# Down projection of a SwiGLU layer: a fourth quarter of the first pair's columns computed with seven block products instead of eight

## The chip, the cores and the metric

The kernel runs on one core of one Trainium2 chip. The metric is the time of one execution on the device in microseconds (us), the median of the runs; the reference's inputs and outputs are float32. A profile of one execution shows what every engine did: TensorE (PE, matmuls; PEld its weight loads), VectorE (DVE), ScalarE (ACT), GpSimd (POOL) and SyncE (SP, which here only starts transfers).

## The reference

One layer on x of 256 rows by 2048 columns. It has five parts, of which two are alike and concern the change:

```
x = x + 0.5 * swiglu(rms_norm(x, ffn1_norm), w_gate, w_up, w_down)     # first half FFN
...                                                                    # S5 state space and stick-breaking attention, one projection out
x = x + 0.5 * swiglu(rms_norm(x, ffn2_norm), w_gate, w_up, w_down)     # second half FFN
...                                                                    # gated embedding

def swiglu(h, w_gate, w_up, w_down):
    return (silu(h @ w_gate) * (h @ w_up)) @ w_down
```

The hidden width of an FFN is 5632, so the down projection is a product of 256 x 5632 by 5632 x 2048.

## The kernel before

**How a product is made exact enough.** TensorE multiplies float32 data in a rounded form ("fp32r"). Each operand is split into a rounded part and a remainder: ScalarE casts (hi), VectorE subtracts (lo), in `split` (lines 182 and 185). A product is hi*hi + lo*hi + hi*lo, so three matmuls for each 128 rows of the sum. The activations are the stationary operand (128x128), the weights the moving one (128 rows by 512 columns).

**How the down projection is tiled.** The sum over 5632 goes in eleven "k quarters" of 512 rows, numbered 0 to 10. The 2048 columns go in four blocks of 512, taken in two pairs (`for n in range(0, ND, 2)`): first the pair of blocks 0 and 1, then 2 and 3. The 256 rows of the activations are two tiles of 128. So a quarter and a pair form a 2x2 by 2x2 product of blocks: two row tiles and two halves of the quarter (256 rows each) against those two halves and two column blocks. There are two ways to compute it, both of class `Seven` (line 501):

- `column` (line 660), "c" in a plan: eight block products, four for each column block. Each weight tile of a quarter (raw, 128x2048) is loaded by SP (line 343), split in two halves, and every half is multiplied with both row tiles. 48 matmuls of 128x512, four splits of weights.
- `chunk` (line 635), "s" in a plan: seven block products after Winograd's form of Strassen's scheme. Both weight tiles are loaded (line 557); VectorE forms three sums of their blocks (`add`, line 550); one more sum is made in place by an adding transfer that POOL starts (line 643); seven splits follow, and 42 matmuls (lines 539, 542, 544). On the side of the activations it needs four sums of the quarter's blocks, made by `sum_forms` (line 487): four VectorE operations of 128x256 (line 496) and one split of 128x1024. A plan's "f" makes those sums ahead of their use.

The products of "c" are added up in banks 2 and 4 (first column block) and 3 and 8 (second); those of "s" in the same and in the shared banks 1, 5, 6 and 7. After the pair's last "s", `opened` (line 811) reads the shared banks: one copy on ScalarE (line 814), and on VectorE two additions (lines 815 and 820) and six gathers into x (line 809). After the pair's last quarter, `end` (line 846) gathers banks 2 and 4, then 3 and 8 into x, and the next norm's `block` transposes x on VectorE (line 220).

**What sets the order.** A plan per pair, in `plans` (line 824), written by hand, gives the order of the quarters. The instructions are then placed on the engines' queues by the framework's scheduler, which also moves them within the limits of the data. Every engine works through its own queue in order. Buffers turn around in pools: five raw tiles, of which x holds two in this stage; four pairs whi/wlo and three pairs shi/slo for split weights (`weight_pair`, line 316, takes them alternately); two for a quarter's split activations (`halves("h")`, tiles hhi and hlo, held by `kept`); four for the split sums of activations and for the next norm's output (`halves("n")`, tiles nhi and nlo); two for sums (tag "sum"). VectorE and ScalarE work ahead of TensorE as far as these pools allow.

**Which sums are kept.** `summed` (line 839) returns a quarter's sums of activations, made at first use. In the first pair (n = 0) the sums for 0 are given back after use, the others are kept for the second pair; in the second pair all are given back.

The two FFNs run the same code, so both down stages follow the same plans.

Of the kernel before, what the change touches and what calls it, by code (L numbers as in the profile page):

```python
# [33 lines left out]
def layer_kernel(ctx: ExitStack, tc: tile.TileContext, a: dict, shapes: dict, out: bass.AP):  # L34
# [47 lines left out]
    def small(n=8):  # L82
        return smp.tile([P, 8], F32, tag="sm", name=uid("sm"))[:, :n]
# [391 lines left out]
    def whole_rows(pool, parts, pinned=False):  # L475

        hi, lo = parts
        u = pool.tile([P, 2, NB], F32, tag="sum", name=uid("whole"), bufs=2)
        added = nc.vector.tensor_tensor(
            out=u.rearrange("p j n -> p (j n)"), in0=hi.bitcast(F32).rearrange("p j t -> p (j t)"),  # L480
            in1=lo.bitcast(F32).rearrange("p j t -> p (j t)"), op=ALU.add,
        )
        if pinned:
            pin(added)
        return u.rearrange("p j n -> p (j n)").rearrange("p (j x b) -> p j x b", j=4, b=32)

    def sum_forms(pool, u, kind="n"):

        sums = pool.tile([P, 2, NB], F32, tag="sum", name=uid("rows"), bufs=2)
        s = sums.rearrange("p j n -> p (j n)").rearrange("p (z j x b) -> p z j x b", z=4, j=2, b=32)  # L490
        (a11, a21), (a12, a22) = ([u[:, k : k + 2, 4 * t : 4 * t + 4] for t in range(TT)] for k in (0, 2))
        for z, (x, y, op) in enumerate((
            (a21, a22, ALU.subtract), (s[:, 0], a11, ALU.subtract),
            (a11, a21, ALU.subtract), (a12, s[:, 1], ALU.add),
        )):
            nc.vector.tensor_tensor(out=s[:, z], in0=x, in1=y, op=op)
        both = halves(kind)
        split(*both, sums.rearrange("p j n -> p (j n)").rearrange("p (z t) -> p z t", z=4))
        return both
# [175 lines left out]
    def ffn(i, xn, nxt, bg=None):  # L675
# [26 lines left out]
        for f in range(NF):  # L702
# [9 lines left out]
            if f >= early or f in alone:  # L712
# [17 lines left out]
                s = Seven(xn, lambda kb: sums[kb], ((wg, f * NB), (wu, f * NB)), sevens, turns)  # L730
# [69 lines left out]
        def rows(k):  # L800
            return hT[k // 2][:, k % 2 * 4 : k % 2 * 4 + 4]
# [9 lines left out]
        def opened(s, n):  # L811
# [10 lines left out]
            gather(xt[1][n + 1], one, -0.5)  # L822

        plans = (
            (("c", 3), ("c", 4), ("s", 0), ("c", 5), ("c", 6), ("s", 1), ("c", 7), ("c", 8), ("s", 2), ("c", 9), ("c", 10)),
            (
                ("c", 10), ("c", 9), ("s", 2), ("c", 3), ("s", 1), ("f", 0), ("c", 4), ("s", 0), ("a", (5, 6, 7, 8)),
            ),
# [1 line left out]
        parts, forms = {}, {}  # L830
# [8 lines left out]
        def summed(kb):  # L839
            if kb not in forms:  # L840
                forms[kb] = sum_forms(sevens, rows(kb))
            return forms.pop(kb) if kb == 0 or n else forms[kb]

        for n in range(0, ND, 2):

            def end(side):
                m = n + side
                for t, z in enumerate(((2, 4), (3, 8))[side]):
                    gather(xt[t][m], s.bank(z), 0.5)
                put_off(0 if m == ND - 2 or m == ND - 1 and m < nxt.early else 2, nxt.block, m)  # L850

            s = Seven(kept, summed, ((wd, n * NB), (wd, (n + 1) * NB)), sevens, turns)
            plan = plans[n // 2]
            left = sum(kind == "s" for kind, _ in plan)
            for kind, kb in plan:
                final = (kind, kb) == plan[-1]
                if kind == "f":
                    forms[kb] = sum_forms(sevens, rows(kb))
                    continue
                if kind == "s":  # L860
                    left -= 1
                    s.chunk(kb, () if left else shared)
                    if not left:
                        put_off(0, opened, s, n)
                    continue
                for side in range(2):
                    s.column(side, (kb,) if kind == "c" else kb[:: 1 - 2 * side], final)
                    if final:
                        end(side)
# [738 lines left out]

    n1, nm, n2, npl = Normed("ffn1_norm", load_turned), Normed("mix_norm"), Normed("ffn2_norm", kinds="hhnn", late=0), Normed("ple_norm", late=0)
    ffn(1, n1, nm, s5_prep)  # L1610

    w_in = a["w_in"]
# [6 lines left out]
    forms = {}  # L1619
# [68 lines left out]
    mix.close()  # L1688

    ffn(2, n2, npl)  # L1690


# [62 lines left out]
    with sums_phase("sums3") as sevens:  # L1755
        forms = {1: sum_forms(sevens, whole_rows(sevens, npl(1)), "h")}
        s = Seven(npl, forms.get, ((wg, 0), (wg, NB)), sevens, sevens)
# [16 lines left out]
    n = ND - 1  # L1774
# [14 lines left out]
    s = small(1)  # L1789
# [157 lines left out]
```

## Time and profile before

| | |
|---|---|
| median of 3 runs | 1810.87 us (1810.7 to 1810.97) |
| the profiled execution | 1810.19 us, of which 1808.4 us from the first to the last instruction |
| granted clock of TensorE | 1.00 |
| first down stage, both pairs | about 472 to 703 us |
| second down stage, both pairs | about 1471 to 1702 us |
| read from HBM / written | 372.41 MB / 10.88 MB |

Times in the profile are microseconds from the span's start. A row of a timeline has the start, the length, the engine, the line, the operation with its result and operands by the program's names, shapes, and, in brackets, how long the engine stood idle before it and who ended that. A row of waits has who waited for whom, the sum, how often and the longest. Matmuls overlap in the profile, so the time one costs is read from start to start. In the names, "acc" and "aux" are banks of TensorE's results; whi/wlo and shi/slo are split weights; sum, weight sums; rows, the sums of activations; mid, the transposed x.

### The profile page before, as it was taken

How to read it: one execution, taken by the hardware profiler on the slowest of the kernel's cores; microseconds unless marked ns; L12 is line 12 of the kernel's file. 1: busy time of each engine (PE TensorE's matmuls, PEld its weight loads, DVE VectorE, ACT ScalarE, POOL GpSimd, SP SyncE). 2: the span in 40 equal slices, each digit the busy share in tenths (PEclk: the TensorE clock that was granted, in tenths of full speed). 3: DMA queues.
4: the chain of work that ended last, by engine and by line, in shares of the span. 5: the costliest groups of instructions: out<-in, count | busy, mean ns of one | idle time of the engine just before them, and what ended most of it. 6: DMA issues, size and time to landing. Idle time of an engine off the chain costs nothing.

```text
span 1808.4 us, 24260 instructions
## 1 busy us (share of the span) xinstructions
PE 1802.4 (100%) x8902; PEld 1494.8 (83%) x8902; DVE 1598.6 (88%) x1872; ACT 1077.4 (60%) x1255; POOL 132.4 (7%) x194
## 2 busy tenths in 40 slices
PE   9999999999999999999999999999999999999998
PEld 8888888888888888888898888888888888888887
DVE  7998889999998897887767899999999999889875
ACT  7545456556565665466895666555565656556664
POOL 0020100000000001122121000000000000000000
PEclk9999999999999999999999999999999999999999
DMA  9689967787776666765646777776777786666663
GB/s 378 213 277 321 276 219 236 244 271 217 252 278 209 207 231 225 249 242 184 205 148 210 246 278 244 258 259 227 233 232 252 237 270 243 223 207 221 203 245 128
DMA packets 108232, 429.46 MB, mean 237 GB/s; under 512 B 24561, under 2 KB 48401, under 8 KB 65713
## 3 DMA queue, kind: packets, MB, share of 16 engines
q1 hardware_dynamic: 95952, 390.10, 61.1%
q0 software_dynamic: 11872, 37.50, 9.6%
q8 instruction: 70, 1.15, 0.3%
q14 instruction: 50, 0.40, 0.1%
q10 hardware_dynamic: 288, 0.31, 0.1%
HBM read 372.41 MB, written 10.88 MB: 212 GB/s over the span
## 4 chain that ended last, share of the span: by engine, by line
PE 99%; DVE 0%; issue 0%; POOL 0%; ACT 0%; DVEq 0%; POOLq 0%
PE acc L358 32%; PE acc L353 16%; PE aux L358 15%; PE aux L353 8%; PE acc L539 5%; PE acc L544 5%; PE acc L542 5%; PE aux L542 3%; PE aux L544 3%; PE aux L539 3%; PE aux L1325 0%; PE acc L1582 0%; PE acc L1577 0%; PE acc L1573 0%; PE aux L1270 0%; PE aux L252 0%
## 5 line engine op out<-in xcount | busy, mean ns | idle before, releaser
L185 DVE TENSOR_TENSOR wlo<-raw,whi 128x1024 fp32r<-128x1024 f32 x478 | 577.6, 1223 | 99.0 <-ACT whi L182 94.1
L182 ACT CAST whi<-raw 128x1024 fp32r<-128x1024 f32 x478 | 495.4, 1050 | 274.0 <-PE acc L358 150.7
L358 PE MATMUL acc<-whi,nhi 128*128 128x512 f32 x852 | 332.7, 392 | 0.1
L358 PE MATMUL acc<-whi,nlo 128*128 128x512 f32 x852 | 330.6, 390 | 0.0
L353 PE MATMUL acc<-wlo,nhi 128*128 128x512 f32 x852 | 241.4, 390 | 0.0
L185 DVE TENSOR_TENSOR slo<-raw,shi 128x1024 fp32r<-128x1024 f32 x186 | 226.8, 1219 | 16.2 <-ACT shi L182 15.6
L182 ACT CAST shi<-raw 128x1024 fp32r<-128x1024 f32 x186 | 195.4, 1050 | 62.1 <-DMA raw<-in_ffn_w_down 24.3
L358 PEld LDWEIGHTS acc<-whi,nhi 128*128 128x128 f32 x852 | 159.9, 188 | 34.1 <-issue 0.5
L353 PEld LDWEIGHTS acc<-wlo,nhi 128*128 128x128 f32 x852 | 159.7, 188 | 33.7 <-DVE wlo L185 0.3
L358 PEld LDWEIGHTS acc<-whi,nlo 128*128 128x128 f32 x852 | 160.0, 188 | 32.5
L182 ACT CAST whi<-sum 128x1024 fp32r<-128x1024 f32 x79 | 83.3, 1054 | 158.3 <-DVE sum L550 141.6
L182 ACT CAST shi<-sum 128x1024 fp32r<-128x1024 f32 x59 | 62.2, 1054 | 102.2 <-DVE sum L550 95.3
L643 POOL DMA_DIRECT2D raw<-raw x45 | 39.2, 871 | 1042.3 <-DVE sum L550 737.6
L550 DVE TENSOR_TENSOR sum<-sum,raw 128x1024 f32<-128x1024 f32 x92 | 112.4, 1222 | 0.9
L185 DVE TENSOR_TENSOR wlo<-sum,whi 128x1024 fp32r<-128x1024 f32 x79 | 96.5, 1223 | 4.8 <-ACT whi L182 4.1
L358 PE MATMUL aux<-whi,nhi 128*128 128x512 f32 x244 | 95.1, 390 | 0.0
L358 PE MATMUL aux<-whi,nlo 128*128 128x512 f32 x244 | 95.0, 389 | 0.0
L353 PE MATMUL aux<-wlo,nhi 128*128 128x512 f32 x244 | 75.2, 389 | 0.0
L185 DVE TENSOR_TENSOR slo<-sum,shi 128x1024 fp32r<-128x1024 f32 x59 | 72.1, 1223 | 1.2 <-ACT shi L182 0.5
L358 PE MATMUL acc<-whi,hlo 128*128 128x512 f32 x156 | 60.9, 390 | 0.0
L358 PE MATMUL acc<-whi,hhi 128*128 128x512 f32 x156 | 60.7, 389 | 0.0
L550 DVE TENSOR_TENSOR sum<-raw,raw 128x1024 f32<-128x1024 f32 x46 | 56.2, 1222 | 3.7 <-DMA raw<-in_ffn_w_down 3.7
(420 smaller groups left out, 3533.3 us busy)
## 6 DMA issues: line engine op xcount, KB each, us to landing
raw<-in_ffn_w_down SPq DMA_DIRECT2D x88, 1024.0 KB, 4.9
raw<-in_ffn_w_gate SPq DMA_DIRECT2D x87, 1024.0 KB, 7.1
raw<-in_ffn_w_up SPq DMA_DIRECT2D x87, 1024.0 KB, 5.4
raw<-in_w_in SPq DMA_DIRECT2D x32, 1024.0 KB, 5.1
raw<-raw POOLq DMA_DIRECT2D x48, 512.0 KB, 5.9
raw<-in_w_out SPq DMA_DIRECT2D x16, 1024.0 KB, 4.9
raw<-in_w_ple_gate SPq DMA_DIRECT2D x16, 1024.0 KB, 5.1
hT<-mid SPq DMA_DIRECT2D x160, 64.0 KB, 4.5
```

What stands on the lines that cost most here:

```text
L182: copy = nc.scalar.copy(hi, src)
L185: rest = nc.vector.tensor_tensor(out=lo, in0=src, in1=hi.bitcast(F32), op=ALU.subtract)
L353: nc.tensor.matmul(ps[t], lhsT=lh, rhs=lo[:, j, cols], start=False, stop=stop and j == 1)
L358: nc.tensor.matmul(ps[t], lhsT=(ahi, alo)[i][:, 2 * h + j, t * P : (t + 1) * P], rhs=hi[:, j, cols], start=start and j == 0 and i == 0, st ...
L539: nc.tensor.matmul(ps, lhsT=lh[j], rhs=hi[:, j], start=begin and j == 0, stop=False, skip_group_check=joined)
L542: nc.tensor.matmul(ps, lhsT=ll[j], rhs=hi[:, j], start=False, stop=False, skip_group_check=joined)
L544: nc.tensor.matmul(ps, lhsT=lh[j], rhs=lo[:, j], start=False, stop=z in final and j == 1, skip_group_check=joined)
L550: nc.vector.tensor_tensor(out=t, in0=x, in1=y, op=ALU.add)
L643: nc.gpsimd.dma_start(b12, b22, accum_op=ALU.add)
```

## The change

The first pair's plan has a fourth "s": quarter 9 is computed with seven products instead of eight. The third "s", quarter 2, comes one quarter sooner, ahead of quarter 8. The sums of activations for 9 are made (by an "f") ahead of quarter 8, and given back after use, as only the first pair uses them. The second pair's plan and everything else stay.

```
         plans = (
-            (("c", 3), ("c", 4), ("s", 0), ("c", 5), ("c", 6), ("s", 1), ("c", 7), ("c", 8), ("s", 2), ("c", 9), ("c", 10)),
+            (
+                ("c", 3), ("c", 4), ("s", 0), ("c", 5), ("c", 6), ("s", 1), ("c", 7), ("s", 2), ("f", 9), ("c", 8), ("s", 9),
+                ("c", 10),
+            ),
...
         def summed(kb):
             if kb not in forms:
                 forms[kb] = sum_forms(sevens, rows(kb))
-            return forms.pop(kb) if kb == 0 or n else forms[kb]
+            return forms.pop(kb) if n or kb in (0, 9) else forms[kb]
```

The three added lines move all later lines of the file by three. Now what it moves on the engines, in the first FFN. First the loads of weights that SP starts, from quarter 7 of the first pair to quarter 10; line 343 loads a tile for a "c", line 557 for an "s". Before:

```order
L343 DMA raw_4747<-in_ffn_w_down 128x2048
L343 DMA raw_4781<-in_ffn_w_down 128x2048
L343 DMA raw_4819<-in_ffn_w_down 128x2048
L343 DMA raw_4853<-in_ffn_w_down 128x2048
L557 DMA raw_4887<-in_ffn_w_down 128x2048
L557 DMA raw_4889<-in_ffn_w_down 128x2048
L343 DMA raw_4985<-in_ffn_w_down 128x2048
L343 DMA raw_5029<-in_ffn_w_down 128x2048
L343 DMA raw_5067<-in_ffn_w_down 128x2048
L343 DMA raw_5103<-in_ffn_w_down 128x2048
```

The same place now:

```order
L343 DMA raw_4747<-in_ffn_w_down 128x2048
L343 DMA raw_4781<-in_ffn_w_down 128x2048
L557 DMA raw_4815<-in_ffn_w_down 128x2048
L557 DMA raw_4817<-in_ffn_w_down 128x2048
L343 DMA raw_4922<-in_ffn_w_down 128x2048
L343 DMA raw_4956<-in_ffn_w_down 128x2048
L557 DMA raw_4990<-in_ffn_w_down 128x2048
L557 DMA raw_4992<-in_ffn_w_down 128x2048
L343 DMA raw_5079<-in_ffn_w_down 128x2048
L343 DMA raw_5125<-in_ffn_w_down 128x2048
```

The number of loads stays; the two of quarter 2 come ahead of quarter 8's, and quarter 9's two are a group's now.

Then VectorE after the last split of quarter 7. Before, quarter 8 begins here: raw_4819 and raw_4853 are its tiles, hT_715 its activations, raw_4887 and raw_4889 those of quarter 2.

```order
L185 TENSOR_TENSOR wlo_4822<-raw_4819,whi_4821 128x1024
L185 TENSOR_TENSOR hlo_4816<-hT_715_3976,hhi_4815 128x1024
L185 TENSOR_TENSOR slo_4826<-raw_4819,shi_4825 128x1024
L185 TENSOR_TENSOR wlo_4856<-raw_4853,whi_4855 128x1024
L185 TENSOR_TENSOR wlo_4860<-raw_4853,whi_4859 128x1024
L185 TENSOR_TENSOR slo_4908<-raw_4887,shi_4907 128x1024
L550 TENSOR_TENSOR sum_4904<-raw_4887,raw_4889 128x1024
```

Now quarter 2 is being worked on there (raw_4815 and raw_4817), and these are the rows from its third sum to the first split of quarter 8 (raw_4922); rows_4909 are the sums of activations for quarter 9:

```order
L550 TENSOR_TENSOR sum_4867<-sum_4855,raw_4815 128x1024
L185 TENSOR_TENSOR slo_4880<-raw_4815,shi_4879 128x1024
L496 TENSOR_TENSOR rows_4909<-hT_715_3976 128x256
L185 TENSOR_TENSOR wlo_4870<-sum_4867,whi_4869 128x1024
L185 TENSOR_TENSOR wlo_4890<-raw_4817,whi_4889 128x1024
L496 TENSOR_TENSOR rows_4909<-rows_4909,hT_715_3976 128x256
L496 TENSOR_TENSOR rows_4909<-hT_715_3976 128x256
L496 TENSOR_TENSOR rows_4909<-hT_715_3976,rows_4909 128x256
L185 TENSOR_TENSOR slo_4900<-raw_4817,shi_4899 128x1024
L185 TENSOR_TENSOR nlo_4915<-rows_4909,nhi_4914 128x1024
L185 TENSOR_TENSOR hlo_4919<-hT_715_3976,hhi_4918 128x1024
L185 TENSOR_TENSOR wlo_4925<-raw_4922,whi_4924 128x1024
```

The sums for 9 stand among the last splits of group 2.

Last, VectorE around the end of the first pair. x_4231 and x_4232 are the two row tiles of x; acc_4255 and acc_4262 are banks 2 and 4, aux_4291 banks 3 and 8; raw_5179, raw_5221 and raw_5259 before are the second pair's tiles of quarter 10 (second column block) and of quarter 9.

```order
L185 TENSOR_TENSOR slo_5186<-raw_5179,shi_5185 128x1024
L809 SCALAR_TENSOR_TENSOR x_4231<-acc_4255,x_4231 128x512
L220 STREAM_TRANSPOSE mid_5163<-x_4231 128x4x4x32
L809 SCALAR_TENSOR_TENSOR x_4232<-acc_4262,x_4232 128x512
L185 TENSOR_TENSOR wlo_5224<-raw_5221,whi_5223 128x1024
L220 STREAM_TRANSPOSE mid_5163<-x_4232 128x4x4x32
L185 TENSOR_TENSOR wlo_5228<-raw_5221,whi_5227 128x1024
L809 SCALAR_TENSOR_TENSOR x_4231<-aux_4291,x_4231 128x512
L809 SCALAR_TENSOR_TENSOR x_4232<-aux_4291,x_4232 128x512
L220 STREAM_TRANSPOSE mid_5163<-x_4231 128x4x4x32
L220 STREAM_TRANSPOSE mid_5163<-x_4232 128x4x4x32
L185 TENSOR_TENSOR slo_5262<-raw_5259,shi_5261 128x1024
```

Now, with raw_5201 in the place of raw_5179 and raw_5243 in that of raw_5221:

```order
L185 TENSOR_TENSOR wlo_5204<-raw_5201,whi_5203 128x1024
L809 SCALAR_TENSOR_TENSOR x_4232<-sg_5101,x_4232 128x512 x2
L809 SCALAR_TENSOR_TENSOR x_4231<-acc_4255,x_4231 128x512
L809 SCALAR_TENSOR_TENSOR x_4232<-acc_4262,x_4232 128x512
L220 STREAM_TRANSPOSE mid_5185<-x_4231 128x4x4x32
L220 STREAM_TRANSPOSE mid_5185<-x_4232 128x4x4x32
L185 TENSOR_TENSOR slo_5208<-raw_5201,shi_5207 128x1024
L185 TENSOR_TENSOR wlo_5246<-raw_5243,whi_5245 128x1024
L809 SCALAR_TENSOR_TENSOR x_4231<-aux_4291,x_4231 128x512
L809 SCALAR_TENSOR_TENSOR x_4232<-aux_4291,x_4232 128x512
L220 STREAM_TRANSPOSE mid_5185<-x_4231 128x4x4x32
L220 STREAM_TRANSPOSE mid_5185<-x_4232 128x4x4x32
```

The last split of the second pair's quarter 10 (slo_5208) stood ahead of the gathers and stands behind the first two of them; the second split of the first tile of quarter 9 (before wlo_5228, ahead of the last two gathers) comes behind them too.

## The prediction

> **What bounds the kernel now.** The first view is the page: its header, the busy times, and the chain of work that ended last.
>
> ```profile
> span 1808.4 us, 24260 instructions
> PE 1802.4 (100%) x8902; PEld 1494.8 (83%) x8902; DVE 1598.6 (88%) x1872; ACT 1077.4 (60%) x1255; POOL 132.4 (7%) x194
> PE 99%; DVE 0%; issue 0%; POOL 0%; ACT 0%; DVEq 0%; POOLq 0%
> ```
>
> TensorE is busy for the whole span and the chain lies on it: a matmul taken away is time taken away, as long as TensorE never has to wait for its operands. VectorE at 88% is the engine that can make it wait. Busy matmuls overlap in the profile, so prices come from start to start. The second view is the timeline of TensorE in the first down stage: the first matmul of quarters 7, 8, 2 (as seven products), 9 and 10.
>
> ```profile
> 534.67 0.39 PE L358 MATMUL acc<-whi,hhi 128*128 128x512 f32 x1
> 545.55 0.39 PE L358 MATMUL acc<-whi,hhi 128*128 128x512 f32 x1
> 556.43 0.39 PE L539 MATMUL acc<-shi,hhi 128*128 128x512 f32 x1
> 565.95 0.39 PE L358 MATMUL acc<-shi,hhi 128*128 128x512 f32 x1
> 576.83 0.39 PE L358 MATMUL acc<-shi,hhi 128*128 128x512 f32 x1
> ```
>
> A plain quarter takes 10.88 us (48 matmuls), a quarter as seven products 9.52 us (42 matmuls): 0.2267 us for a matmul in both, so nothing stalls between them. The third view is the busy time by stretch. The rows are: quarter 7 to the end of the first pair; the second pair's quarters 10 and 9; its groups up to the start of quarters 5 to 8; and the same three in the second FFN. The columns are length, PE, PEld, DVE, ACT, POOL, clock, DMA share, GB/s.
>
> ```profile
> 534.67:587.71 53.04, 53.04 (x235) 43.95 (x234) 43.26 (x43) 29.19 (x33) 0.88 (x1) 1.00 0.66 230
> 587.71:609.47 21.76, 21.76 (x97) 18.03 (x96) 18.31 (x20) 12.29 (x18) 0.86 (x1) 1.00 0.56 148
> 609.47:659.79 50.32, 50.32 (x223) 41.70 (x222) 47.24 (x48) 35.13 (x40) 1.74 (x2) 1.00 0.72 240
> 1533.64:1586.68 53.04, 53.04 (x236) 43.93 (x234) 43.67 (x44) 29.54 (x33) 0.87 (x1) 1.00 0.66 230
> 1586.68:1608.44 21.76, 21.76 (x98) 18.02 (x97) 18.13 (x20) 12.18 (x18) 0.85 (x1) 1.00 0.52 132
> 1608.44:1658.76 50.32, 50.32 (x224) 41.68 (x223) 47.62 (x48) 32.49 (x37) 1.73 (x2) 1.00 0.70 239
> ```
>
> PE fills every stretch. VectorE is free for 53.04 - 43.26 = 9.78 us at the end of the first pair and for 3.45 us in the next two quarters; in the second FFN for 9.37 and 3.63 us. After that it is nearly full (50.32 - 47.24 = 3.08 us, and 2.70 us).
>
> **The change part by part. TensorE.** In each of the two FFNs quarter 9 goes from 48 matmuls to 42: 6 x 0.2267 = 1.36 us less, on the path; twice that is 2.72 us. [...]
>
> **VectorE.** Per FFN it gets three sums of weight blocks (L550), three more remainders of splits (seven instead of four), four quarter-size sums of rows (L496) and their remainder: seven operations on 128x1024 and four on 128x256. Prices are from start to start, where it has no idle time:
>
> ```profile
> 633.06 0.42 DVE L496 TENSOR_TENSOR rows<-hT 128x256 f32<-128x256 f32 x1
> 633.39 0.42 DVE L496 TENSOR_TENSOR rows<-hT,rows 128x256 f32<-128x256 f32 x1
> 633.73 1.22 DVE L185 TENSOR_TENSOR hlo<-hT,hhi 128x1024 fp32r<-128x1024 f32 x1
> 634.86 1.23 DVE L185 TENSOR_TENSOR wlo<-raw,whi 128x1024 fp32r<-128x1024 f32 x1
> 636.00 1.22 DVE L185 TENSOR_TENSOR nlo<-rows,nhi 128x1024 fp32r<-128x1024 f32 x1
> 637.13 1.22 DVE L185 TENSOR_TENSOR slo<-raw,shi 128x1024 fp32r<-128x1024 f32 x1
> ```
>
> That is 7 x 1.135 + 4 x 0.335 = 9.29 us. The stretch is also 1.36 us shorter, so VectorE needs 10.65 us of idle time. It has 9.78 + 3.45 = 13.23 us of it before the second pair's first group of seven, 13.00 in the second FFN. So 2.58 and 2.35 us are left, and I cost the work at nothing. Whether this idle time can be used depends on why it is there; the next rows are who waited for whom in the first stretch.
>
> ```profile
> DVE wlo L185 <- ACT whi L182: 5.1, 5, 1.5
> ACT shi L182 <- PE acc L358: 5.0, 4, 1.7
> ACT whi L182 <- PE acc L358: 4.5, 4, 1.7
> ACT shi L182 <- PE aux L358: 4.2, 3, 1.7
> DVE slo L185 <- ACT shi L182: 3.9, 3, 1.5
> ACT whi L182 <- PE aux L358: 3.6, 3, 1.7
> ACT whi L182 <- DMA raw<-in_ffn_w_down: 3.1, 3, 2.3
> ```
>
> 9.0 of the 9.78 us are VectorE waiting for ScalarE's casts, and ScalarE in turn waited 17.3 us for TensorE to free the split weights' buffers and 3.1 us for a load. So most of it is a full pool: VectorE is as far ahead as it can get. Such idle time can be filled without anyone noticing.
>
> How far ahead that is shows at the last split of group 2, in the first pair and in the second, each with its matmul, and at the tightest place of the second pair; the sixth row is the next norm's work inside the second pair:
>
> ```profile
> 557.30 1.23 DVE L185 TENSOR_TENSOR wlo<-raw,whi 128x1024 fp32r<-128x1024 f32 x1 [1.49 <-ACT whi L182]
> 565.50 0.62 PE L544 MATMUL aux<-wlo,nhi 128*128 128x512 f32 x2
> 610.35 1.23 DVE L185 TENSOR_TENSOR wlo<-raw,whi 128x1024 fp32r<-128x1024 f32 x1 [1.54 <-ACT whi L182]
> 618.54 0.39 PE L544 MATMUL aux<-wlo,nhi 128*128 128x512 f32 x1
> 651.36 1.23 DVE L185 TENSOR_TENSOR wlo<-sum,whi 128x1024 fp32r<-128x1024 f32 x1 [1.12 <-ACT whi L182]
> 617.75 1.67 DVE L197 SCALAR_TENSOR_TENSOR nlo<-h,gains,nhi 128x256 fp32r<-128x256 f32 x4
> 655.26 0.61 PE L544 MATMUL acc<-wlo,hhi 128*128 128x512 f32 x2
> ```
>
> The lead, from the split's end to the matmul's start, is 565.50 - 558.53 = 6.97 and 618.54 - 611.58 = 6.96 us at the ends of groups, equal because the pool is full there, and 655.26 - 652.59 = 2.67 us at the tightest place. Followed through the new order: group 2 ends at up to 6.97 again. The sums for 9 (4 x 0.335 + 1.135 = 2.5 us) leave 4.5. Quarter 8 (four remainders and one of the activations, 5.7 us against PE's 10.88) brings 9.7. Group 9 (three sums, seven remainders, one of the activations: 11 x 1.135 = 12.5 against 9.52) leaves 6.7. Quarter 10 with the eight half-size operations of the banks' reading (0.605 each by the gathers below: 5.7 + 4.8 = 10.5 against 10.88) 7.1, the next two quarters with their 3.45 us free 10.5. The second pair's group 2 (12.5 and 1.6 for the norm, against 9.52) ends at 5.9, where it ended at 6.96. So some 1.1 us of lead are missing from there on, and 2.67 becomes an estimated 1.6 us at the tightest place: TensorE still doesn't wait.
>
> **ScalarE, POOL, buffers.** ScalarE gets four casts more:
>
> ```profile
> 558.12 1.05 ACT L182 CAST shi<-raw 128x1024 fp32r<-128x1024 f32 x1
> ```
>
> At most 4 x 1.05 = 4.2 us, of 53.04 - 29.19 = 23.9 us free: nothing. POOL gets one 512 KB adding transfer per FFN. The sums for 9 take a pair of the four "n" buffers while 1 and 2 hold two; they leave after group 9, before the next norm asks: nothing.
>
> **What is moved.** SP's order of loads swaps quarter 8 and group 2, so the two raw tiles of group 9 come only one quarter behind those of group 2. The last gathers of the pair now stand ahead of one more split of the next pair. They wait for TensorE, and in the trace they and the two transposes take this on VectorE:
>
> ```profile
> 587.91 1.29 DVE L809 SCALAR_TENSOR_TENSOR x<-aux,x 128x512 f32<-128x512 f32 x2 [0.86 <-PE aux L353]
> 589.12 1.30 DVE L220 STREAM_TRANSPOSE mid<-x 128x512 f32<-128x512 f32 x2
> ```
>
> Such a set lasts 590.33 - 587.91 = 2.42 us, plus 1.23 for the split behind it. The first set can start when side 0 of quarter 10 ends, 5.44 us before the pair's end, and TensorE wants that split (the last of the next quarter 10) 5.44 + 8.16 + 0.91 = 14.5 us after that. A lead of 10.8 us remains: nothing.
>
> **Sum.** 2 x 1.36 = 2.72 us off the profiled execution's own 1810.19 us (span 1808.4 and 1.8 around it): 1807.47. The median of the runs lies 0.68 higher at 1810.87, so the forecast is 1810.87 - 2.72 = **1808.15 us**, 0.15% less. A measurement of this kernel can tell about 0.2%, 3.62 us, from no change.
>
> **Rivals. The lead isn't won back (slower).** If none of the first stretch's idle time can be filled, say because it only becomes new waits, VectorE is 10.65 - 3.45 - 2.67 = 4.53 us short per FFN by the second pair's tightest place (4.35 with the second FFN's 3.63), and TensorE waits for a remainder there: 8.88 - 2.72 = 6.16 us more, **1817.0**. It turns into a loss when under (4.53 - 1.36) / 9.78 = 32% of that idle time can be used, and into one of over 0.2% under about 14%. For it: in the third stretch VectorE is 94% busy. Against it: the waits above. 6%.
>
> **The weight loads (part of the gain lost).** The loads and the adding transfer in the trace:
>
> ```profile
> raw<-in_ffn_w_down SPq DMA_DIRECT2D x88, 1024.0 KB, 4.9
> DMA to landing us min/median/max: 4.5/5.8/8.9
> ```
>
> x holds two of the five raw buffers in this stage and a group holds two of the other three until its last splits. Group 9's second tile can be asked for only when quarter 8's first tile is split, and lands 4.9 us later; group 9's first sum needs it. ScalarE's longest wait for a load was 2.3 us. With the lead gone, one such wait per FFN would reach TensorE: 2 x 2.3 = 4.6 us back, 1812.8; with half of it, 1810.5. It decides only if the wait outlasts the lead of some 7 us that group 9 starts and ends with; 4.9 us doesn't. [...] 16%.
>
> **The change does less than it says.** A quarter as seven products is measured above at 42 matmuls, and both FFNs use the plan, so I give this nothing. A gain over 3.62 us would need stalls elsewhere to go; there are none in these stages: 2%.
>
> **How the numbers follow.** Full gain 76%, loads 16%, lost lead 6%, a bigger gain 2%. Full gain alone is 1807.8 to 1808.6 (the runs of before spread by 0.27 us). The range reaches down to 1807.4 for the profiled execution's offset, and up to 1810.4, most of the loads' case. Faster by over 0.2%: 0.02. Slower by over 0.2%: half of the lost lead's chance, 0.03. Within 0.2%: 0.95.
>
> **What would show it.** Right: TensorE still busy through both down stages, the first pair 1.36 us shorter, VectorE's busy time there 9.3 us up and its idle time before the second pair gone by about 10.6 us. Wrong: a matmul on wlo or slo with idle time ahead of it between 545 and 660 us (or 1544 and 1660), or a sum (L550) that waits for a raw load by over 2 us with TensorE waiting behind it; or no idle time filled and the second pair longer than now.

## The result and the profile after

The changed kernel takes 1807.82 us, the median of 22 runs (1806.71 to 1809.11). The kernel before takes 1810.68 us beside it (22 runs, 1809.9 to 1812.19). The ratio is 0.9985, 95% interval 0.9978 to 0.9991: 2.86 us less, where the forecast had 2.72. That is 0.15% of the time, and the interval leaves out 1.

The header and the busy times on the page after:

```profile
span 1806.3 us, 24268 instructions
PE 1799.4 (100%) x8890; PEld 1492.0 (83%) x8890; DVE 1615.7 (89%) x1894; ACT 1083.6 (60%) x1263; POOL 134.6 (7%) x196
```

The span is 2.1 us shorter in this one execution. Quarter 7, ahead of which both kernels do the same, begins 0.89 us later in it than before (535.56 instead of 534.67), so the lengths of the stretches say more here than the spans. VectorE's busy time rose by 17.1 us, TensorE's fell by 3.0. The first pair's end in TensorE's timeline after, the first matmuls of quarter 7, group 9, quarter 10 and the second pair:

```profile
535.56 0.39 PE L358 MATMUL acc<-whi,hhi 128*128 128x512 f32 x1
...
566.84 0.39 PE L539 MATMUL acc<-shi,hhi 128*128 128x512 f32 x1
576.36 0.39 PE L358 MATMUL acc<-shi,hhi 128*128 128x512 f32 x1
587.24 0.39 PE L358 MATMUL acc<-shi,hhi 128*128 128x512 f32 x1
```

Quarter 9 takes 576.36 - 566.84 = 9.52 us and the whole stretch 587.24 - 535.56 = 51.68 instead of 53.04: 1.36 us are gone. The stretches of before at their new places, first and second FFN, with the columns as before:

```profile
535.56:587.24 51.68, 51.68 (x230) 42.79 (x228) 50.98 (x53) 33.25 (x37) 1.76 (x2) 1.00 0.68 226
587.24:609.00 21.76, 21.76 (x98) 18.02 (x96) 18.91 (x22) 12.08 (x18) 0.87 (x1) 1.00 0.59 161
609.00:659.32 50.32, 50.32 (x224) 41.67 (x222) 46.55 (x48) 34.54 (x39) 1.78 (x2) 1.00 0.74 251
1533.18:1584.86 51.68, 51.68 (x230) 42.81 (x228) 50.95 (x53) 33.09 (x37) 1.73 (x2) 1.00 0.66 225
1584.86:1606.62 21.76, 21.76 (x98) 18.02 (x96) 18.91 (x22) 12.08 (x18) 0.88 (x1) 1.00 0.58 162
1606.62:1656.94 50.32, 50.32 (x224) 41.68 (x222) 47.38 (x50) 35.26 (x39) 1.73 (x2) 1.00 0.77 255
```

TensorE fills all of them still. VectorE's free time in the first stretch fell from 9.78 us to 0.70, so it is now the engine that is full there. The waits of that first stretch after show the same from the other side:

```profile
ACT whi L182 <- DVE sum L550: 6.5, 4, 4.0
ACT shi L182 <- DVE sum L550: 3.1, 2, 2.9
...
ACT whi L182 <- PE acc L358: 1.3, 1, 1.3
ACT whi L182 <- PE aux L358: 1.0, 1, 1.0
...
DVE sum L550 <- DMA raw<-in_ffn_w_down: 0.3, 1, 0.3
DVE wlo L185 <- ACT whi L182: 0.2, 1, 0.2
```

ScalarE's wait for TensorE's buffers fell from 17.3 us to 2.8 (the two shown and 0.5), VectorE's for ScalarE from 9.0 to 0.2, and ScalarE now waits 9.6 us for VectorE's sums. The pools are no longer full: the idle time of a full pool was filled. What is left as lead shows in two pairs of rows, the last split of group 9 with its matmul, and the tightest place of the second pair (VectorE first, then TensorE, in both):

```profile
567.72 1.23 DVE L185 TENSOR_TENSOR wlo<-raw,whi 128x1024 fp32r<-128x1024 f32 x1 [0.21 <-ACT whi L182]
652.02 1.22 DVE L185 TENSOR_TENSOR slo<-sum,shi 128x1024 fp32r<-128x1024 f32 x1
```

```profile
575.91 0.62 PE L544 MATMUL aux<-wlo,nhi 128*128 128x512 f32 x2
654.79 0.61 PE L544 MATMUL acc<-slo,hhi 128*128 128x512 f32 x2
```

The leads are 575.91 - 568.95 = 6.96 us and 654.79 - 653.24 = 1.55 us. No matmul of either down stage waits, and each down stage is 1.36 us shorter, the six matmuls and nothing else.

### The profile page after: what moved, and what is told of

Same layout as the page of the kernel before. It is cut to its first block, busy times and chain, and to the rows that moved or that the text cites. A ratio compares the mean times of both kernels' runs of the same rounds, so it can differ in the third digit from the quotient of the medians.

```text
span 1806.3 us, 24268 instructions
## 1 busy us (share of the span) xinstructions
PE 1799.4 (100%) x8890; PEld 1492.0 (83%) x8890; DVE 1615.7 (89%) x1894; ACT 1083.6 (60%) x1263; POOL 134.6 (7%) x196
## 4 chain that ended last, share of the span: by engine, by line
PE 99%; DMA 0%; DVE 0%; ACT 0%; SPq 0%; issue 0%; DVEq 0%; ACTq 0%
PE acc L358 31%; PE acc L353 16%; PE aux L358 15%; PE aux L353 8%; PE acc L539 5%; PE acc L544 5%; PE acc L542 5%; PE aux L544 4%; PE aux L539 4%; PE aux L542 4%; PE aux L1328 0%; PE acc L1585 0%; PE acc L1580 0%; PE acc L1576 0%; DMA raw<-in_head 0%; PE aux L1273 0%
## 5 line engine op out<-in xcount | busy, mean ns | idle before, releaser
L182 ACT CAST whi<-sum 128x1024 fp32r<-128x1024 f32 x83 | 87.5, 1054 | 166.2 <-DVE sum L550 154.4
L550 DVE TENSOR_TENSOR sum<-sum,raw 128x1024 f32<-128x1024 f32 x96 | 117.1, 1220 | 0.9
L185 DVE TENSOR_TENSOR wlo<-sum,whi 128x1024 fp32r<-128x1024 f32 x83 | 101.2, 1222 | 3.1 <-ACT whi L182 2.2
```

Of the source, the lines that this page charges most:

```text
L182: copy = nc.scalar.copy(hi, src)
L185: rest = nc.vector.tensor_tensor(out=lo, in0=src, in1=hi.bitcast(F32), op=ALU.subtract)
L550: nc.vector.tensor_tensor(out=t, in0=x, in1=y, op=ALU.add)
```

## The experiments

Medians, with the difference to the kernel before, measured beside each. "Waits" are TensorE's in each kernel's one profiled execution: what the starts of two matmuls lie apart above 0.2267 us, added up from distances of 0.32 us on, without the gaps that every kernel's trace has in the same places, where it lacks matmuls. They stand for the first down stage, the second, and the beginning of the embedding behind it (some 1710 to 1730 us, up to 30 us later in the slowest kernels). A ratio's interval is about 0.0009 wide on each side, 1.6 us (0.0014 in e4 and e6), and the difference of two rows of this table is uncertain by some 2 us.

| kernel | median us | to before | ratio, 95% interval | waits, us |
|---|---|---|---|---|
| the kernel before | 1810.68 | | | 0; 0.2; 0.1 |
| the change | 1807.82 | -2.86 | 0.9985 [0.9978, 0.9991] | 0; 0; 0.2 |
| e7_six_less | 1808.32 | -2.29 | 0.9985 [0.9976, 0.9994] | 0; 0; 1.0 |
| e1_first_ffn | 1809.55 | -1.06 | 0.9992 [0.9983, 1.0001] | 0; 0; 0.3 |
| e2_move_alone | 1810.56 | -0.05 | 1.0001 [0.9992, 1.0009] | 0; 0; 1.1 |
| e3_group_in_place | 1814.70 | +4.09 | 1.0025 [1.0015, 1.0035] | 2.9; 2.4; 1.3 |
| e9_sums_at_use | 1807.50 | -3.07 | 0.9984 [0.9975, 0.9993] | 0; 0; 0.1 |
| e8_more_traffic | 1810.14 | -0.47 | 1.0000 [0.9991, 1.0008] | 0.1; 0.2; 1.3 |
| e10_one_again | 1809.82 | -0.75 | 0.9997 [0.9988, 1.0006] | 0; 0; 4.9 |
| e11_one_again_first | 1808.57 | -2.00 | 0.9987 [0.9978, 0.9996] | 0; 0; 0 |
| e12_one_again_second | 1809.11 | -1.46 | 0.9992 [0.9983, 1.0001] | 0; 0; 2.4 |
| e5_two_again | 1812.50 | +1.89 | 1.0010 [1.0001, 1.0019] | 1.4; 1.6; 2.1 |
| e4_fifth_group | 1828.16 | +17.55 | 1.0098 [1.0084, 1.0112] | 10.9; 10.9; 0.8 |
| e6_eleven_again | 1837.24 | +26.63 | 1.0146 [1.0132, 1.0160] | 14.7; 12.1; 1.3 |

### Does VectorE's work cost anything? e7 and e1

e7 is the kernel before without one of quarter 9's eight block products (first pair, both FFNs). It takes the six matmuls away and adds nothing for VectorE.

```
+                        if (kb, half[0], t) in skip:
+                            continue
...
+                s.column(side, (kb,) if kind == "c" else kb[:: 1 - 2 * side], final, [(9, 0, 0)] if n + side == 1 else ())
```

> The kernel before with one block product of quarter 9 left out in each FFN (row tile 0, first half of the quarter, second column block): 6 matmuls less per FFN, nothing added on VectorE. Theory (VectorE's work of the change costs nothing): the same time as the change, 1807.8, 2.7 us under before. Rivals (the work or the loads cost something, hidden in the net gain): faster than the change by what they cost, up to 4.6 us.

Measured: -2.29 us, ratio 0.9985, the change's own. So the 9 us of VectorE's work for each FFN cost nothing that these intervals can tell. The first part of the theory stands.

e1 is the change in the first FFN only.

```
+            if i == 2 and n == 0:
+                plan = (("c", 3), ("c", 4), ("s", 0), ("c", 5), ("c", 6), ("s", 1), ("c", 7), ("c", 8), ("s", 2), ("c", 9), ("c", 10))
```

> The change in the first FFN alone; the second keeps the old plan. Theory (six matmuls of 0.2267 us less per FFN, VectorE's extra work in idle time): half of the gain, 1.36 us under before, first FFN's last five quarters of the first pair 51.68 us and the second FFN's 53.04. Rival (the lead isn't won back, so that something is lost in one FFN and the gain comes from elsewhere): all of the 2.8 us or nothing of it.

Measured: -1.06 us. It agrees with half the gain, though its interval reaches just past 1. In its profile the first FFN's stretch from quarter 7 on takes 51.67 us and the second's 53.04, as expected.

### What the move is for: e2, e3, e9

e2 is the kernel before with quarter 2 one quarter sooner, e3 the change with group 9 right behind group 2, e9 the change without "f".

```
-   ("c", 7), ("c", 8), ("s", 2), ("c", 9), ("c", 10)),                  # before
+   ("c", 7), ("s", 2), ("c", 8), ("c", 9), ("c", 10)),                  # e2
-   ("c", 7), ("s", 2), ("f", 9), ("c", 8), ("s", 9), ("c", 10),         # the change
+   ("c", 7), ("c", 8), ("s", 2), ("s", 9), ("c", 10),                   # e3
+   ("c", 7), ("s", 2), ("c", 8), ("s", 9), ("c", 10),                   # e9
```

> Quarter 2's group moved one quarter sooner, quarter 9 still plain: as many matmuls and as much work on VectorE as before. Theory: no difference from before (within 0.5 us). Rival (part of the gain is the new place of group 2): up to 2.8 us less than before.

Measured: -0.05 us. The move alone is free and brings nothing.

> Four groups, but without the move and without the sums made ahead: 7, 8 plain, then groups 2 and 9 back to back, then 10. Same instructions as the change. Theory by lead, quarter by quarter: group 2 ends with a lead of at most 6.97 us because the pool is full, group 9 with its sums costs VectorE 15.0 us against 9.52 (lead 1.5), quarter 10 and the next two bring some 3.8 (5.3), the second pair's group 2 takes 4.6 (0.7) and the way to the tightest place 4.3: TensorE waits about 3.6 us per FFN, so 4.5 us over before. If only the sum of the idle time counted: as the change, 2.8 us under before.

Measured: +4.09 us. The same work on the same engines, with the groups back to back, costs 7 us more than the change. So the sum of idle time over the whole stretch isn't what decides. The ledger of the lead gave the size of the loss (+4.5), but not its way. It had 1.5 us of lead at the end of group 9 and 0.7 at the end of the second pair's group 2; e3's trace has 574.86 - 572.15 = 2.71 us and 617.01 - 610.86 = 6.15 us there. By then the lead was back. It is lost right behind, at the second pair's quarter 3, whose first tile lands late. The rows for that tile, before, in the change and in e3 (SP first, then ScalarE's cast and VectorE's split; before, neither waits for the tile):

```profile
605.67 0.53 SPq L343 DMA_DIRECT2D raw<-in_ffn_w_down  x1
```

```profile
591.08 0.33 SPq L557 DMA_DIRECT2D raw<-in_ffn_w_down  x1
591.45 16.64 SPq L233 DMA_DIRECT2D h<-mid  x22
608.20 0.53 SPq L343 DMA_DIRECT2D raw<-in_ffn_w_down  x1
614.05 2.00 ACT L182 CAST whi<-raw 128x1024 fp32r<-128x1024 f32 x2 [3.27 <-DMA raw<-in_ffn_w_down]
615.14 1.23 DVE L185 TENSOR_TENSOR wlo<-raw,whi 128x1024 fp32r<-128x1024 f32 x1 [2.90 <-ACT whi L182]
```

```profile
593.47 17.44 SPq L233 DMA_DIRECT2D h<-mid  x24
611.01 0.53 SPq L343 DMA_DIRECT2D raw<-in_ffn_w_down  x1
616.45 2.00 ACT L182 CAST whi<-raw 128x1024 fp32r<-128x1024 f32 x2 [5.45 <-DMA raw<-in_ffn_w_down]
617.53 1.22 DVE L185 TENSOR_TENSOR wlo<-raw,whi 128x1024 fp32r<-128x1024 f32 x1 [4.75 <-ACT whi L182]
```

In these rows SP starts its transfers one after another. Quarter 3's load stands behind the small transfers of the next norm (h<-mid, 0.7 to 0.8 us each; in the change 22 of them up to 608.09 us, and the load 0.11 us later), and these stand behind the load of group 2's second tile (L557 in the change's rows). In the change that load waits 1.3 us for a split of VectorE (slo, up to 591.04) and starts at 591.08 us; before, it starts at 587.96, 0.10 us behind four of h<-mid, without a wait for a split, and in e3 at 593.09. So VectorE's late splits at the pair's end come back as a late load 17 us on, and VectorE then stands idle for 2.90 us in the change and 4.75 in e3, with little idle time behind it to win the lead back. This is read from the traces; no run here moves those transfers. TensorE's row at one of its waits in e3:

```profile
668.75 1.21 PE L353 MATMUL acc<-wlo,hhi 128*128 128x512 f32 x4 [0.68 <-DVE wlo L185]
```

VectorE's row for the split it waits for, in e3:

```profile
667.48 1.22 DVE L185 TENSOR_TENSOR wlo<-raw,whi 128x1024 fp32r<-128x1024 f32 x1
```

The matmul starts 0.05 us behind the split's end (668.70), over 90 us behind group 9: the price falls due at the second pair's tight places.

> The change without its "f": the sums of activations for quarter 9 are made when group 9 begins, not ahead of quarter 8; the same work on every engine. By the lead ledger they only move behind quarter 8's splits: the lead there is 9.7 + 2.5 = 12.2 us if no pool caps it, and about 7 if one does, so the 2.5 us of the sums fit either way and TensorE doesn't wait: within 0.5 us of the changed kernel (about 1807.9). Rival: the first matmul of group 9 needs a sum of activations, and what stands ahead of it on VectorE (three weight sums, the row sums, their remainder: 3 x 1.135 + 2.5 = 5.9 us) with the wait for the second raw tile eats the lead of some 7: a wait of 1 to 2 us for each FFN, +2 to +4 us over the changed kernel.

Measured: -3.07 us, the change's time again. Making the sums ahead of quarter 8 or at their use is the same, so of the plan's two novelties only the quarter between the groups matters. e9 is the shortest of all kernels here, by 0.2 us that its interval doesn't separate from the change.

### How much cover is left: e5, e6, e10, e11, e12, e4

In e5, e6 and e10 VectorE computes two, eleven or one remainder from group 9 on twice, at 1.135 us each, in both FFNs (the group has eight, so e6's last three belong to quarter 10); in e11 and e12 one, in the first or the second FFN. The values don't change. But the scheduler also puts some of VectorE's later operations in another order in these kernels, so they aren't the change with time added and nothing else.

```
             rest = nc.vector.tensor_tensor(out=lo, in0=src, in1=hi.bitcast(F32), op=ALU.subtract)
+            if repeat[0]:
+                repeat[0] -= 1
+                rest = nc.vector.tensor_tensor(out=lo, in0=src, in1=hi.bitcast(F32), op=ALU.subtract)
...
+                    repeat[0] = 2 if kb == 9 else 0      # e6: 11; e10: 1; e11: 1, and i != 2; e12: 1, and i == 2
```

> The change with two remainders of group 9 computed twice on VectorE (same values): 2.27 us more of VectorE's time per FFN, nothing on TensorE. Theory: 2.58 us of idle time and a lead of about 1.5 us are left, so 0 to 1.4 us over the change in all. Rival (VectorE is already the bound): 4.5 us over the change.

Measured: +1.89 us, which is 4.75 above the change; expected were 0 to 1.4, and the rival had 4.5. TensorE's rows at the waits in e5 (lines are one to four further down in these kernels):

```profile
656.12 0.73 PE L548 MATMUL acc<-slo,hhi 128*128 128x512 f32 x2 [0.66 <-DVE slo L186]
1634.34 0.72 PE L548 MATMUL acc<-slo,hhi 128*128 128x512 f32 x2 [0.81 <-DVE slo L186]
1655.26 0.73 PE L548 MATMUL acc<-wlo,hhi 128*128 128x512 f32 x2 [0.21 <-DVE wlo L186]
1725.67 0.50 PE L362 MATMUL acc<-whi,nhi 128*128 128x512 f32 x1 [1.42 <-ACT whi L183]
```

The first three are the second pair's tight places. The waits of the first down stage sum to 1.4 us and those of the second to 1.6, for 2.27 us more of VectorE in each. That isn't the repeat alone. Quarter 3's load starts at 610.36 us here (608.20 in the change), so VectorE stands idle for 3.77 us ahead of it. And in the first FFN a split of activations stands ahead of the split that TensorE waits for at 656.12; in the change it stands behind it:

```profile
653.71 1.22 DVE L186 TENSOR_TENSOR hlo<-hT,hhi 128x1024 fp32r<-128x1024 f32 x1
654.85 1.22 DVE L186 TENSOR_TENSOR slo<-sum,shi 128x1024 fp32r<-128x1024 f32 x1
```

The last of the four rows above is another place: the embedding's first product, behind the second FFN.

> The changed kernel with one remainder of group 9 computed twice (1.135 us more VectorE work for each FFN), to bound how much cover the change leaves. By the lead at the tightest place (1.54 us in the changed kernel's first FFN, 1.93 in its second), 0.4 us are left there, and it costs nothing: within 0.6 us of the changed kernel. Rival, pro rata from two remainders twice (+4.7): +2.3 us, because the place behind the second FFN, where the lead is 0.06 us, passes on any delay of VectorE.

> The changed kernel with one remainder of group 9 computed twice in the first FFN only (1.135 us of VectorE). In both FFNs together it cost about 2 us, though the profile had no TensorE wait in either down stage; all of it stood where the embedding begins, behind the second FFN, where a load of the gate's weights took 8.4 us to land instead of 5.4. If only that place pays, the first FFN's repeat costs nothing: within 0.7 us of the changed kernel (about 1807.8). Rival: every us of VectorE is paid in its own FFN: about +1.0 us here.

> The same in the second FFN only. If the place where the embedding begins pays for VectorE work of the FFN ahead of it, the whole excess of about 2 us over the changed kernel is here (about 1809.8). Rival, each FFN pays its own: about +1.0. If neither this nor the first alone costs anything, the excess comes from nothing that the repeat delays, but from the spread of that load's landing time between executions and kernels.

Measured: e10 2.1 us above the change, e11 0.9 and e12 1.4. By the medians e10 and e11 lie at their rivals' figures (2.3 and 1.0) and e12 between the two, but the intervals don't tell expectation from rival: runs of e10 lie between 1808.39 and 1812.91 us. The profiles say something else. None of the three has a wait in a down stage, so in these executions one remainder for each FFN is covered there; with e5, the cover of the down stages lies between 1.1 and 2.3 us. e11, without a wait in any of the three places, has the shortest span of all (1805.6 us); this execution took 0.8 us less than e11's median. In e10 and e12 all waits stand at the embedding's beginning. TensorE's timeline there in e10, whose profiled execution took 1812.91 us, the longest of its runs:

```profile
1721.43 0.61 PE L548 MATMUL aux<-wlo,hhi 128*128 128x512 f32 x2
1724.17 0.79 PE L362 MATMUL acc<-whi,nhi 128*128 128x512 f32 x1 [2.12 <-ACT whi L183]
1724.76 0.63 PE L362 MATMUL acc<-whi,nlo 128*128 128x512 f32 x1
1725.19 0.63 PE L362 MATMUL acc<-whi,nhi 128*128 128x512 f32 x1
```

The cast it waits for waits for a load in turn. SP's row for that load and ScalarE's for the cast, first in e10, then in the change:

```profile
1714.60 0.53 SPq L347 DMA_DIRECT2D raw<-in_w_ple_gate  x1
1723.07 1.04 ACT L183 CAST whi<-raw 128x1024 fp32r<-128x1024 f32 x1 [5.28 <-DMA raw<-in_w_ple_gate]
```

```profile
1714.22 0.53 SPq L343 DMA_DIRECT2D raw<-in_w_ple_gate  x1
1719.52 1.05 ACT L182 CAST whi<-raw 128x1024 fp32r<-128x1024 f32 x1 [3.07 <-DMA raw<-in_w_ple_gate]
```

From issue to cast it is 8.47 us in e10 and 5.30 in the change, with the load asked for 0.4 us later and SP's order there the same. The change has hardly any lead at that place (its first matmul starts at 1720.86, 0.3 us behind the cast's end), so a load that lands 3 us late holds TensorE up for most of that. In e12 a weight sum and its cast come late there instead, and the matmul behind them waits 1.14 us at 1716.54.

Whether the repeat causes these delays or such delays come and go between executions is open: each kernel has one profile, and e2 and e7, which add no work there, have 1.1 and 1.0 us of waits there too.

> The same with eleven remainders from group 9 on computed twice: 12.5 us more per FFN. Theory: all but the left-over cover of 2.6 to 4.1 us per FFN shows, 17 to 20 us over the change. If there were cover left that the ledger doesn't see: under 12 us. Rival (no cover at all): 25 us.

Measured: 29.5 us above the change, more than the 2 x 11 x 1.135 = 25.0 us that were added; expected were 17 to 20. Something came on top, then. Stretches of e6 with the granted clock (the third column from the right), from a wait of 2.07 us on:

```profile
591.30:594.10 2.80, 2.80 (x8) 2.24 (x7) 2.80 (x3) 1.59 (x5) 0.00 (x0) 0.50 0.20 38
594.30:600.00 5.70, 5.70 (x27) 4.70 (x26) 4.61 (x7) 2.75 (x5) 0.00 (x0) 1.00 0.93 362
```

Here TensorE itself runs at half its clock for some 3 us, and its matmuls stand 0.43 us apart. This happens behind two of e6's waits, at some 1.5 us each; and each of its some 30 waits costs 0.11 us more than its own length, in the one matmul behind it. Without these, some 22 us of waits are left in its profile for the 25.0 added: about 3 us were covered in both FFNs together, where 2.6 to 4.1 for each were expected.

> Quarter 8 as seven products too (five groups in the first pair; 2, 8 and 9 in a row): 6 matmuls less per FFN again, 9.3 us more on VectorE. Theory: the cover is used up. VectorE needs 21.3 us of idle time per FFN and has 13.2 and a lead of 2.7 us: at least 5.4 us of waits per FFN against 2.72 gained, so 5 us over before or more, to 13 us over where full pools waste idle time. If the work were free: 5.4 us under before.

The fifth group is quarter 8:

```
-   ("c", 7), ("s", 2), ("f", 9), ("c", 8), ("s", 9), ("c", 10),
+   ("c", 7), ("s", 2), ("s", 8), ("f", 9), ("s", 9), ("c", 10),
...
-            return forms.pop(kb) if n or kb in (0, 9) else forms[kb]
+            return forms.pop(kb) if n or kb in (0, 8, 9) else forms[kb]
```

Measured: +17.55 us, 20.4 above the change; expected were 5 to 13 over the kernel before. A fifth group takes another 9.29 + 1.36 = 10.65 us of VectorE's time for each FFN, 21.3 us in both, and the profile has 22.6 us of waits, with what waits cost on top: nearly all of it shows. In this place a fifth group doesn't pay; other places weren't tried.

### The loads: e8

The change with two more 512 KB writes for each FFN, started by POOL behind the sums for 9.

```
+                    if kb == 9:
+                        for side, part in enumerate(forms[kb]):
+                            nc.gpsimd.dma_start(scr_more[side], part.bitcast(F32).rearrange("p z t -> p (z t)"))
```

> The change with two transfers of 512 KB more per FFN: the split sums for quarter 9 are written to memory while group 9's weights are loaded. Theory: a load that lands 2 to 4 us later is covered by the lead of 5 to 7 us: the time of the change within 0.7 us. Rival (the weight loads are what is tight): each FFN loses 2 to 4 us, 4 to 8 us over the change.

Measured: 2.4 us above the change. That lies between what theory (within 0.7) and rival (4 to 8) expected. In its profile the down stages have 0.3 us of waits and the embedding's beginning 1.3 us, so the loads of group 9 are covered even with that traffic. What makes up the rest of the median isn't shown.

## Why the prediction was right

**TensorE's six matmuls**: right. The first pair is 53.04 - 51.68 = 1.36 us shorter in both FFNs, 0.2267 us for a matmul at a granted clock of 1.00. The difference of the medians, 2.86 us with some 1.2 us on either side, agrees with 2.72, but is too wide to check the price of a matmul by itself.

**VectorE's work at nothing**: right. e7 shows it as far as its interval goes, and the trace more sharply: no matmul of the down stages waits. VectorE's idle time before the second pair's first group of seven fell from 13.23 to 0.70 + 2.85 = 3.55 us, by 9.7 where 10.6 was forecast, and in the second FFN from 13.00 to 0.73 + 2.85 = 3.58, by 9.4. Its busy time rose by 17.1 / 2 = 8.55 us for each FFN where 9.29 was worked out, and in the first stretch alone by 50.98 - 43.26 = 7.72 us. One reason is in the rows: an operation with idle time ahead counts its full 1.22 us, one right behind another 1.135, so every gap that closes takes 0.085 off.

**The lead**: right at two ends, and by another way between them. Group 9 ends with 6.96 us where 6.7 was worked out, and the tightest place keeps 1.55 where it was 1.6. But the step that took 1.1 us off, the second pair's group 2 that "ends at 5.9, where it ended at 6.96", failed. The group's last split and its matmul, after:

```profile
609.88 1.22 DVE L185 TENSOR_TENSOR slo<-raw,shi 128x1024 fp32r<-128x1024 f32 x1 [0.41 <-ACT shi L182]
618.07 0.39 PE L544 MATMUL aux<-slo,nhi 128*128 128x512 f32 x1
```

The lead is 618.07 - 611.10 = 6.97 us. What is missing at the tightest place is lost behind that, in the 2.90 us for which VectorE waits for quarter 3's tile (shown with e3); the ledger had no load in it. That it came out at 1.6 is luck in part. e10 points the same way: with 1.135 us more of VectorE's work its lead at that place is larger, 654.56 - 652.03 = 2.53 us, as VectorE stands idle for only 0.80 us ahead of quarter 3. In the change's second FFN the idle time there is 2.37 us and the lead at the tightest place 1.92.

**What is left over**: wrong, with no effect on the time. The step "So 2.58 and 2.35 us are left" took what remains of the idle time for cover. e5 shows that 2.27 us more aren't covered, and e10's profile that 1.135 are. The idle time after is even 3.55 us, but 2.85 of it comes behind the first pair's end, where VectorE stands for casts and loads.

**ScalarE and POOL at nothing**: right. ScalarE's busy time in the stretch rose by 33.25 - 29.19 = 4.06 us of the 4.2 allowed, POOL's by one transfer.

**The loads** (rival, 16%): fell at group 9. The one wait of a sum for a load in that stretch is 0.3 us, at a share of the DMA engines of 0.68 instead of 0.66. Nor did e8's writes make these loads come last: its profile has 0.3 us of TensorE's waits in both down stages. But late loads are what takes the lead in the second pair. In the first FFN ScalarE's waits for loads there grow from 1.0 us to 7.7, of which 7.0 are these:

```profile
ACT whi L182 <- DMA raw<-in_ffn_w_down: 7.0, 3, 3.3
```

None of them reaches TensorE in the change.

**The lost lead** (rival, 6%): fell for this change. Its condition was that idle time can't be filled; 9.7 us of it were, for each FFN. Waits of its kind, for a remainder in the second pair, are what e3, e5, e6 and e4 show once group 9 comes too early or the work grows.

**Not foreseen**: the embedding's beginning, where the first remainder is ready only some 0.05 us ahead of its matmul, before and after. It was left out of the ledger, which ended with the second pair. It costs 0.1 us before and 0.2 after, so nothing of the gain; in e10, e12 and e5 it costs 2 to 5.

## What to carry to other kernels

Look for idle time of an engine that feeds another and stands for full buffers: here 9.7 us of VectorE's were filled for each FFN, and no matmul of the down stages waited. Follow the lead from one stage to the next through the new order, since the same total of work cost 7 us more with the two heavy groups side by side. Take the loads into that ledger: here a load that waited for its buffer started at 591.08 us instead of 587.96, the load 17 us behind it at 608.20 instead of 605.67, and VectorE then stood idle for 2.90 us. The sum of the remaining idle time isn't cover; here it was over 3 us, and 2.3 us more of work weren't covered. And end the ledger not at the stage that was changed but at the next place where the lead is near nothing.

## What the runs showed of the hardware

In these traces a wait cost TensorE more than its length. The matmul behind a wait stands some 0.34 us from its successor instead of 0.23, behind 0.28 us of idle time (e8's matmul at 1715.95: 0.34) as behind 3.20 us (e4's at 1577.02: 0.35), where the clock doesn't drop at once. And the clock did drop behind some: in e4 (3.36 us, and 0.70 behind it), e6 (2.07 and 2.15) and e10 (2.29) matmuls come 0.43 us apart for some 3 us, at once or up to 1.8 us after the wait's end, at a granted clock of 0.54 in e4 (1579.40 to 1581.60 us), 0.50 in e6's stretch above and here in e10:

```profile
1724.80:1727.50 2.70, 2.70 (x8) 2.12 (x7) 2.70 (x5) 2.70 (x7) 0.00 (x0) 0.50 0.45 173
```

It isn't the length alone. This wait of e6, as long as those (2.45 us by the same measure), is followed at full pace:

```profile
628.84 0.50 PE L362 MATMUL acc<-whi,hhi 128*128 128x512 f32 x1 [2.29 <-ACT whi L183]
629.17 0.40 PE L362 MATMUL acc<-whi,hlo 128*128 128x512 f32 x1
629.41 0.39 PE L362 MATMUL acc<-whi,hhi 128*128 128x512 f32 x1
```

So waits of 2.07 to 2.29 us within busy stretches were followed by the half clock and one of 2.45 us was not; the traces don't show what tells them apart.
